# Score products of a differential attention: the low part of q over 64 rows, both softmax halves side by side in two PSUM banks

## The chip, the cores and the metric

The kernel runs on one core of one Trainium2 chip. The metric is the device time of one execution in microseconds (us); lower is better. TensorE (PE, with its weight loader PEld), VectorE (DVE), ScalarE (ACT), GpSimd (POOL) and SyncE (SP, which issues nearly all DMAs) work side by side, each through its own stream of instructions, in the order that was fixed when the kernel was compiled.

## The reference

One layer of a hybrid decoder trunk with 1024 tokens and a width of 1024. A combined input projection gives q, k, v, a convolution branch and gates. The part that matters here is the differential attention, with 8 heads, each with two softmax halves of 64 dimensions, and v of 128:

```python
q = rms_norm(q.reshape(B, S, N_HEADS, 2, HEAD_DIM), q_norm_w[l])
k = rms_norm(k.reshape(B, S, N_HEADS, 2, HEAD_DIM), k_norm_w[l])
...
def probs(qb, kf):
    s = jnp.einsum('bhqd,bhkd->bhqk', qb, kf) * scale + bias
    s = jnp.where(causal, s, -jnp.inf)
    return jax.nn.softmax(s, axis=-1)

p = probs(qb1, k1f) - lamf * probs(qb2, k2f)
return jnp.einsum('bhqk,bhkd->bhqd', p, vf)
```

Behind it come a norm, the convolution branch, the gated merge, an output projection and a SwiGLU feed-forward part, all in float32.

## The kernel before

Every large product is made from rounded operands: a value is split into a high part (what the fast float32 type of TensorE holds) and a low part (the residual), and the product is the sum of high x high, high x low and low x high (`mm3`, L152 to L155, out tiles `pg`, `pW`, `wo`).

The work has stages. Up to about 328 us the first input projections run (V, U, the first Q items). From 328 to about 834 us the attention runs: for each head h and each block i of 128 queries `scores(h, i)` (L865) makes the scores of (i+1) x 128 keys for both halves, `turn` (L903) transposes the probabilities of the step before, `weigh` (L924) multiplies them with v. Between these, `more` issues the remaining projections (Q and G items, tiles `pg`) as filling work, `slot` issues the later parts of earlier steps, and `bg.step` gives VectorE a few taps of the convolution (L542). From 834 us on follow the two branch projections, the output projection and the feed-forward part.

The order of instructions on each engine is set by a planner at compile time: it goes through the program in order of priority, and an instruction whose buffer or operand is not yet there (by the planner's own estimate of times) is passed by later ones that are ready.

Layout of q and k. `q_item` projects one head's q and k, and `turn_qk` (L737) transposes 512 tokens of each, so that the 128 rows of a tile hold the 64 dimensions of the first half and the 64 of the second. L751 writes the high parts into `s1`, L753 the low parts into `lo`. DMAs from SBUF to SBUF (L754, L760, L761, L759 for q; L754, L764, L765 for k) then move rows:

- for k, `s1` becomes [high of half 1; low of half 1] and `s2` [low of half 2; high of half 2], 64 rows each;
- for q, `s1` becomes the high part of half 1 twice, `s2` the high part of half 2 twice, and `lo` and `lo2` the same for the low parts.

So one product over all 128 rows gives (q high) x (k high + k low), and a second one (q low) x (k high + k low). `scores` makes a tile `sc` for each half j and each chunk of at most 512 keys: L883 is the product with q's high part, L884 adds the one with q's low part, and L885 on VectorE adds the bias, writes the sum to `E` and keeps the running minimum. There are three PSUM banks for `sc`. Behind the chunks of one half comes its exponential on ScalarE (L890), and behind both halves VectorE's L896 to L900 combine them. The chunks of the eight blocks are

```python
SPLITS = [[128], [256], [384], [512], [512, 128], [512, 256], [512, 384], [512, 512]]
```

which makes 12 chunks for each head and half, 192 tiles in all.

Other TensorE lines that the prediction names: L693 is a small product over 33 rows (rows of the bias table), L236 eight transposes of 31 rows (the convolution's weights), L673 the projection of v, L744 the transposes of q and k.

Of the kernel before, what the change touches and what calls it, by code (L numbers as in the profile page):

```python
# [10 lines left out]
F32 = mybir.dt.float32  # L11
F32R = mybir.dt.float32r
AF = mybir.ActivationFunctionType
# [3 lines left out]
P = 128  # L17
S = 1024
D = 1024
H = 8  # L20
HD = 64
# [36 lines left out]
def kernel(  # L58
# [28 lines left out]
    dve, act, pool, pe = nc.vector, nc.scalar, nc.gpsimd, nc.tensor  # L87
# [24 lines left out]
    def nm(s):  # L112
        uid[0] += 1
        return f"{s}_{uid[0]}"

    def f32(ap):
        return ap.bitcast(F32)
# [4 lines left out]
    last_lo, last_mm = [None], [None]  # L122
# [16 lines left out]
    def pg():  # L139
        npg[0] += 1  # L140
        p_, tag = pgs[npg[0] % len(pgs)]
        return p_.tile([P, 512], F32, tag=tag, name=nm("pg"))
# [4 lines left out]
    def pm(z="pm"):  # L147
        npm[0] += 1
        p_, tag = pms[npm[0] % len(pms)]
        return p_.tile([P, 512], F32, tag=tag, name=nm(z))  # L150
# [28 lines left out]
    one = ap.tile([1, P], F32, name="one", bufs=1)  # L179
# [14 lines left out]
    def pcol(key, k=0):  # L194
        c = col[key] + k
        return pvec[:, c : c + 1]
# [143 lines left out]
    def gemm_T(w, mhi, mlo, sb, amid=None):  # L340

        o = pg()
        cs = slice(sb * 512, (sb + 1) * 512)
        for k in range(NKT):
            mm3(o[:], w[0][:, k, :], w[1][:, k, :], kt(mhi, k)[:, cs], kt(mlo, k)[:, cs], k == 0, k == NKT - 1)
            if amid is not None and k == NKT // 2 - 1:
                amid()
        return o

    def gemm_N(o, halves, shi, slo, i):  # L350

        ts = slice(i * P, (i + 1) * P)
        for k in range(NKT):
            whi, wlo = halves[k // 4]
            mm3(o, kt(shi, k)[:, ts], kt(slo, k)[:, ts], whi[:, k % 4, :], wlo[:, k % 4, :], k == 0, k == NKT - 1)
# [265 lines left out]
    def rstd_of(ss, n, scale, fast=False):  # L621
        v = sm.tile([P, 16], F32, tag="v", name=nm("v"))[:, :n]
        dve.tensor_scalar(v, ss, scale, EPS, op0=ALU.mult, op1=ALU.add)
        return rsq(v, n, fast)
# [81 lines left out]
    def qk_pool():  # L706

        if not pools:
            vw_ctx.close()
            pools["qk"] = qk_ctx.enter_context(tc.tile_pool(name="qkp", bufs=2, side="right", reuse_waits="tile"))  # L710
        return pools["qk"]

    def q_item(h):
        qkp = qk_pool()
        halves = [ws.next(), ws.next()]
        t = {}
        T[h] = t
        for b in range(2):
            raw = qkp.tile([P, 4, 256], F32, tag="qkraw", name=nm("qkraw"), bufs=2)
            ss = sm.tile([P, 16], F32, tag="ss16", name=nm("ss16"))  # L720
            for i2 in range(2):
                o = pg()
                for e in range(2):
                    gemm_N(o[:, 256 * e : 256 * (e + 1)], halves, hT_hi, hT_lo, 4 * b + 2 * i2 + e)
                act.copy(raw[:, 2 * i2 : 2 * i2 + 2, :], o[:].rearrange("p (e c) -> p e c", c=256))
                jk = sm.tile([P, VD], F32, tag="jk", name=nm("jk"), bufs=1)[:, :HD]
                for g in range(8):
                    act.activation(  # L728
                        jk, o[:, g * HD : (g + 1) * HD], AF.Square, accum_out=ss[:, 8 * i2 + g : 8 * i2 + g + 1]
                    )  # L730
                if i2 == 0:
                    yield
            r = rstd_of(ss[:], 16, 1.0 / HD, fast=h > 0)
            r4 = raw[:].rearrange("p i (g d) -> p (i g) d", d=HD)
            dve.tensor_tensor(r4, r4, r.unsqueeze(2).to_broadcast([P, 16, HD]), op=ALU.mult)

            def turn_qk(b=b, raw=raw):  # L737


                dma = nc.sync.dma_start  # L740
                for z, key in enumerate(("q", "k")):
                    pt = pm("pQ")
                    for i in range(4):
                        pe.transpose(pt[:, i * P : (i + 1) * P], raw[:, i, z * P : (z + 1) * P], ident[:])  # L744
                    w = pcol(key + "n")

                    def part(j):
                        return qkp.tile([P, 512], F32R, tag=f"{key}s{j}", name=f"{key}s{j}_{h}_{b}", bufs=2 if key == "q" else 3)

                    s1, s2 = part(1), part(2)  # L750
                    act.activation(s1[:], pt[:], AF.Identity, scale=w)  # L751
                    lo = part(3) if key == "q" else qkp.tile([P, 512], F32R, tag="klo", name=f"klo_{h}_{b}", bufs=1)
                    dve.scalar_tensor_tensor(lo[:], pt[:], w, f32(s1[:]), op0=ALU.mult, op1=ALU.subtract)  # L753
                    dma(f32(s2[HD:, :]), f32(s1[HD:, :]))  # L754
                    if key == "q":
                        lo2 = part(4)
                        for one, two in ((s1, s2), (lo, lo2)):
                            if one is lo:
                                dma(f32(two[HD:, :]), f32(one[HD:, :]))  # L759
                            dma(f32(two[:HD, :]), f32(one[HD:, :]))  # L760
                            dma(f32(one[HD:, :]), f32(one[:HD, :]))  # L761
                        t["q", b] = (s1, lo), (s2, lo2)
                    else:
                        dma(f32(s2[:HD, :]), f32(lo[HD:, :]))  # L764
                        dma(f32(s1[HD:, :]), f32(lo[:HD, :]))  # L765
                        t["k", b] = s1, s2

            late.append((NT * h if b and h else 0, turn_qk))
            yield

# [71 lines left out]
    aps = at_ctx.enter_context(tc.tile_pool(name="attn", bufs=2, reuse_waits="tile"))  # L842
    psc = at_ctx.enter_context(tc.tile_pool(name="psc", bufs=1, space=PSUM))
    pms.extend([(ps, "pm"), (psc, "pm2")])

    SPLITS = [[128], [256], [384], [512], [512, 128], [512, 256], [512, 384], [512, 512]]
# [18 lines left out]
    def scores(h, i):  # L865

        t, tb = T[h], TB[h]
        nk = (i + 1) * P
        mn = sm.tile([P, 2], F32, tag="mn", name=nm("mn"))
        l = sm.tile([P, 2], F32, tag="l", name=nm("l"))  # L870
        E = []
        qs = slice(i % 4 * P, (i % 4 + 1) * P)
        for j in range(2):
            qh, ql = t["q", i // 4][j]
            e = aps.tile([P, S], F32, tag="E", name=nm("E"), bufs=4)
            E.append(e)
            c0 = 0
            for w in SPLITS[i]:
                ks = slice(c0, c0 + w)
                o = psc.tile([P, 512], F32, tag="sc", name=nm("sc"), bufs=3)  # L880
                kb = c0 // 512
                k = t["k", kb][j][:, :w]
                pe.matmul(o[:, :w], qh[:, qs], k, start=True, stop=False)  # L883
                last_mm[0] = pe.matmul(o[:, :w], ql[:, qs], k, start=False, stop=True).ins  # L884
                dve.tensor_tensor_reduce(  # L885
                    e[:, ks], o[:, :w], tb[:, S - nk + c0 : S - nk + c0 + w], 1.0,
                    mn[:, j : j + 1] if c0 else 3.0e38, ALU.add, ALU.min, accum_out=mn[:, j : j + 1],
                )
                c0 += w
            act.activation(  # L890
                e[:, :nk], e[:, :nk], AF.Exp, bias=mn[:, j : j + 1], scale=-1.0, accum_out=l[:, j : j + 1]
            )
        if h not in RL:
            RL[h] = sm.tile([P, NT], F32, tag="rl1", name=f"rl1_{h}")
        c = sm.tile([P, 1], F32, tag="rl", name=nm("rl"))
        dve.reciprocal(c[:], l[:, 1:2])  # L896
        dve.scalar_tensor_tensor(c[:], c[:], neglam[:], l[:, 0:1], op0=ALU.mult, op1=ALU.mult)
        e1, e2 = E[0][:, :nk], E[1][:, :nk]
        dve.scalar_tensor_tensor(e1, e2, c[:], e1, op0=ALU.mult, op1=ALU.add)
        dve.reciprocal(RL[h][:, i : i + 1], l[:, 0:1])  # L900
        ES[h, i] = E[0]

# [232 lines left out]
    part = bp.tile([P, P], F32, tag="part", name="part", bufs=1)  # L1135
# [50 lines left out]
    for c in range(NE, NKT):  # L1186
        w = ws.next()
# [6 lines left out]
    for cl in ((0, 1, 2), (3, 4), (5, 6), (7,)):  # L1194
        pair = [(c, ws.next()) for c in cl]
        for sb in range(2):
            cs = slice(sb * 512, (sb + 1) * 512)
            for c, w in pair:
# [3 lines left out]
                o = gemm_T(w, cT_hi, cT_lo, sb)  # L1202
# [50 lines left out]
    def wo_bank(t_):  # L1253
        p_, tag = wo_banks[t_]
        return p_.tile([P, 512], F32, tag=tag, name=nm("wo"))
# [8 lines left out]
    for z, (c, ls) in enumerate(WO):  # L1264
        ts_ = [4 * l + i for l in ls for i in range(4)]
        o = {t_: wo_bank(t_) for t_ in ts_}
# [321 lines left out]
```

## Time and profile before

| | |
|---|---|
| Three runs, median (lowest to highest) | 1788.25 us (1786.38 to 1788.89) |
| Profiled execution, span | 1789.3 us, 25085 instructions; no other time of this execution is given |
| TensorE busy in the span | 1753.9 us (98%), 8987 products |
| TensorE weight loads | 1490.4 us (83%) |
| VectorE | 1271.3 us (71%) |
| ScalarE | 804.0 us (45%) |
| Mean granted TensorE clock | 0.991 |
| DMA | 274.77 MB |

A busy time of TensorE counts each product until its modelled end, and successive products overlap; the step from one start to the next tells what a product costs the stream. L12 means line 12 of the kernel. In a row of the time line stand the start, the duration, the engine, the line, the operation, the tiles (out<-in) and the shapes; `64*128` would be a stationary operand of 64 rows and 128 columns. A bracket at the end of a row gives the idle time in front and what ended it; "issue" means that nothing in the profile shows what the engine waited for. In the views of one line or tile stand the number of instructions, durations in ns (lowest/median/highest), and the first and last start.

### The profile page before, as it was taken

The numbers are of one execution on the slowest core, as the hardware profiler recorded it, in microseconds if no ns is written. First come the engines' busy times: TensorE is split into PE (matmuls) and PEld (weight loads), VectorE is DVE, ScalarE is ACT, GpSimd is POOL, SyncE is SP. The second block draws the span as 40 slices with busy tenths as digits, with TensorE's granted clock in tenths as the row PEclk, the third lists the DMA queues.
The fourth block names the chain that finished last, engine by engine and source line by source line (L and its number), as shares of the span: only waits on it lengthen the run. The fifth ranks groups of instructions, "written<-read, shape, count | busy, mean of one in ns | idle before, by whom it ended". The sixth has DMA issues, their size and how long they took to land.

```text
span 1789.3 us, 25085 instructions
## 1 busy us (share of the span) xinstructions
PE 1753.9 (98%) x8987; PEld 1490.4 (83%) x8987; DVE 1271.3 (71%) x2189; ACT 804.0 (45%) x1890; POOL 19.6 (1%) x93
## 2 busy tenths in 40 slices
PE   7899999999999999999999999999999999999999
PEld 5687898988989998987788888878888888888887
DVE  5349888999989898888488533876666766664554
ACT  4221142458767686655447313543333333333333
POOL 0001000000000000000000000000000000000000
PEclk9999999999999999998999999999999999999999
DMA  5337324234343444351793543315454454597663
GB/s 189 97 120 251 118 81 138 73 108 126 109 124 112 131 113 121 98 165 65 258 307 123 165 171 125 117 60 171 143 171 156 154 178 151 184 347 261 219 212 130
DMA packets 249817, 274.77 MB, mean 154 GB/s; under 512 B 16362, under 2 KB 165907, under 8 KB 249692
## 3 DMA queue, kind: packets, MB, share of 16 engines
q1 hardware_dynamic: 248122, 267.47, 46.6%
q0 software_dynamic: 1280, 4.91, 0.9%
q8 instruction: 71, 1.16, 0.3%
q10 hardware_dynamic: 290, 0.79, 0.1%
q14 instruction: 54, 0.44, 0.1%
HBM read 176.07 MB, written 78.68 MB: 142 GB/s over the span
## 4 chain that ended last, share of the span: by engine, by line
PE 90%; DVE 4%; DMA 3%; ACT 2%; issue 1%; SPq 0%; ACTq 0%; DVEq 0%
PE acc L1442 21%; PE pg L153 13%; PE pg L154 13%; PE pg L155 13%; PE acc L468 12%; PE pg L673 5%; PE sc L884 2%; PE wo L155 2%; PE wo L154 2%; PE wo L153 2%; PE sc L883 2%; PE pT L919 1%; PE pW L153 1%; DMA wraw<-in_w_in_dram 1%; PE pW L155 1%
## 5 line engine op out<-in xcount | busy, mean ns | idle before, releaser
L542 DVE SCALAR_TENSOR_TENSOR acc<-u,cw,acc 128x1024 f32<-128x1024 f32 x240 | 306.7, 1278 | 2.5
L153 PE MATMUL pg<-hT_hi,whi 128*128 128x512 f32 x512 | 200.4, 392 | 2.0 <-ACT sgg L580 2.0
L155 PE MATMUL pg<-hT_hi,wlo 128*128 128x512 f32 x512 | 200.9, 393 | 0.0
L154 PE MATMUL pg<-hT_lo,whi 128*128 128x512 f32 x512 | 200.5, 392 | 0.0
L120 ACT CAST whi<-wraw 128x1024 fp32r<-128x1024 f32 x101 | 106.2, 1052 | 188.0 <-PE pg L154 96.5
L125 DVE TENSOR_TENSOR wlo<-wraw,whi 128x1024 fp32r<-128x1024 f32 x101 | 123.1, 1220 | 75.1 <-ACT whi L120 74.8
L125 DVE TENSOR_TENSOR wlo<-draw,whi 128x1024 fp32r<-128x1024 f32 x75 | 91.8, 1224 | 89.0 <-ACT whi L120 83.7
L153 PE MATMUL pg<-whi,hT_hi 128*128 128x256 f32 x512 | 146.3, 286 | 0.0
L154 PE MATMUL pg<-wlo,hT_hi 128*128 128x256 f32 x512 | 145.8, 285 | 0.0
L155 PE MATMUL pg<-whi,hT_lo 128*128 128x256 f32 x512 | 145.7, 285 | 0.0
L120 ACT CAST whi<-draw 128x1024 fp32r<-128x1024 f32 x75 | 79.1, 1055 | 129.5 <-PE acc L468 119.3
L468 PE MATMUL acc<-wlo,whi 128*128 128x512 f32 x308 | 119.8, 389 | 0.0
L468 PE MATMUL acc<-whi,wlo 128*128 128x512 f32 x308 | 119.8, 389 | 0.0
L890 ACT ACTIVATE E<-E,mn 128x256 f32<-128x256 f32 (+7 forms) x128 | 99.5, 779 | 38.8 <-DVE mn L885 37.5
L153 PEld LDWEIGHTS pg<-hT_hi,whi 128*128 128x128 f32 x512 | 96.2, 188 | 21.6 <-ACT sgg L580 2.8
L155 PEld LDWEIGHTS pg<-hT_hi,wlo 128*128 128x128 f32 x512 | 96.2, 188 | 19.9 <-issue 0.6
L154 PEld LDWEIGHTS pg<-hT_lo,whi 128*128 128x128 f32 x512 | 96.2, 188 | 19.4 <-issue 0.6
L153 PEld LDWEIGHTS pg<-whi,hT_hi 128*128 128x128 f32 x512 | 97.6, 191 | 2.1 <-ACT jk L728 0.5
L154 PEld LDWEIGHTS pg<-wlo,hT_hi 128*128 128x128 f32 x512 | 97.6, 191 | 1.4
L155 PEld LDWEIGHTS pg<-whi,hT_lo 128*128 128x128 f32 x512 | 97.6, 191 | 0.9
L1442 PE MATMUL acc<-h_hi,whi 128*128 128x512 f32 x240 | 93.4, 389 | 0.0
L1442 PE MATMUL acc<-h_lo,whi 128*128 128x512 f32 x240 | 93.4, 389 | 0.0
(281 smaller groups left out, 4216.8 us busy)
## 6 DMA issues: line engine op xcount, KB each, us to landing
wraw<-in_w_gate_up_dram SPq DMA_DIRECT2D x44, 512.0 KB, 5.0
wraw<-in_w_in_dram SPq DMA_DIRECT2D x38, 512.0 KB, 3.7
qs<-qs SPq DMA_DIRECT2D x96, 128.0 KB, 2.3
wd<-in_w_down_dram SPq DMA_DIRECT2D x44, 256.0 KB, 3.2
tdT<-wd SPq DMA_DIRECT2D x88, 128.0 KB, 4.4
draw<-sdS SPq DMA_DIRECT2D x44, 256.0 KB, 4.0
draw<-tdT SPq DMA_DIRECT2D x44, 256.0 KB
wraw<-in_w_in_dram SPq DMA_DIRECT2D x32, 256.0 KB, 3.5
```

What stands on the lines that cost most here:

```text
L120: act.copy(dst, src)
L125: last_lo[0] = dve.tensor_tensor(dst, src, f32(hi), op=ALU.subtract).ins
L153: pe.matmul(o, lh, rh, start=start, stop=False)
L154: pe.matmul(o, lh, rl, start=False, stop=False)
L155: last_mm[0] = pe.matmul(o, ll, rh, start=False, stop=stop).ins
L468: m = pe.matmul(o[s_][i][:], l_[:, ts], r_[:, 512:], start=start and j + y_ == 0, stop=j == n - 1 and y_ == 2, skip_group_check=not start,)
L542: dve.scalar_tensor_tensor(acc[0][:], us[c][:, t : t + S], cw[:, c, t : t + 1], acc[0][:], op0=ALU.mult, op1=ALU.add)
L673: last_mm[0] = pe.matmul(o[:], l_, r_, start=n_ == 0, stop=n_ == len(terms) - 1).ins
L883: pe.matmul(o[:, :w], qh[:, qs], k, start=True, stop=False)
L884: last_mm[0] = pe.matmul(o[:, :w], ql[:, qs], k, start=False, stop=True).ins
L890: act.activation(e[:, :nk], e[:, :nk], AF.Exp, bias=mn[:, j : j + 1], scale=-1.0, accum_out=l[:, j : j + 1])
L1442: pe.matmul(o[:], a_[x_][:, k, :], b_[y_][:, k, :], start=start and k + x_ + y_ == 0, stop=k == 3 and x_ == 1, skip_group_check=not start,)
```

## The change

The product with q's low part now runs over 64 rows: `lo` keeps the low part of half 1 in rows 0 to 63 and that of half 2 in rows 64 to 127, as L753 writes it, and it is multiplied with the 64 rows of the k tile that hold k's high part (rows 0 to 63 of `s1`, rows 64 to 127 of `s2`). The product low x low is no longer formed. The tile `lo2` and three DMAs for each q tile go. In `scores` the loops are exchanged: for each chunk both halves' tiles are taken, first the two products with the high part, then the two with the low part, then VectorE's two L885; the two exponentials come behind all chunks.

```diff
                     dve.scalar_tensor_tensor(lo[:], pt[:], w, f32(s1[:]), op0=ALU.mult, op1=ALU.subtract)
                     dma(f32(s2[HD:, :]), f32(s1[HD:, :]))
                     if key == "q":
-                        lo2 = part(4)
-                        for one, two in ((s1, s2), (lo, lo2)):
-                            if one is lo:
-                                dma(f32(two[HD:, :]), f32(one[HD:, :]))
-                            dma(f32(two[:HD, :]), f32(one[HD:, :]))
-                            dma(f32(one[HD:, :]), f32(one[:HD, :]))
-                        t["q", b] = (s1, lo), (s2, lo2)
+                        dma(f32(s2[:HD, :]), f32(s1[HD:, :]))
+                        dma(f32(s1[HD:, :]), f32(s1[:HD, :]))
+                        t["q", b] = (s1, s2), lo
...
-        E = []
+        E = [aps.tile([P, S], F32, tag="E", name=nm("E"), bufs=4) for j in range(2)]
         qs = slice(i % 4 * P, (i % 4 + 1) * P)
-        for j in range(2):
-            qh, ql = t["q", i // 4][j]
-            e = aps.tile([P, S], F32, tag="E", name=nm("E"), bufs=4)
-            E.append(e)
-            c0 = 0
-            for w in SPLITS[i]:
-                ks = slice(c0, c0 + w)
-                o = psc.tile([P, 512], F32, tag="sc", name=nm("sc"), bufs=3)
-                kb = c0 // 512
-                k = t["k", kb][j][:, :w]
-                pe.matmul(o[:, :w], qh[:, qs], k, start=True, stop=False)
-                last_mm[0] = pe.matmul(o[:, :w], ql[:, qs], k, start=False, stop=True).ins
+        qh, ql = t["q", i // 4]
+        rows = slice(0, HD), slice(HD, P)
+        c0 = 0
+        for w in SPLITS[i]:
+            o = [psc.tile([P, 512], F32, tag="sc", name=nm("sc"), bufs=3) for j in range(2)]
+            k = t["k", c0 // 512]
+            for j in range(2):
+                pe.matmul(o[j][:, :w], qh[j][:, qs], k[j][:, :w], start=True, stop=False)
+            for j in range(2):
+                last_mm[0] = pe.matmul(
+                    o[j][:, :w], ql[rows[j], qs], k[j][rows[j], :w], start=False, stop=True
+                ).ins
+            for j in range(2):
                 dve.tensor_tensor_reduce(
-                    e[:, ks], o[:, :w], tb[:, S - nk + c0 : S - nk + c0 + w], 1.0,
+                    E[j][:, c0 : c0 + w], o[j][:, :w], tb[:, S - nk + c0 : S - nk + c0 + w], 1.0,
                     mn[:, j : j + 1] if c0 else 3.0e38, ALU.add, ALU.min, accum_out=mn[:, j : j + 1],
                 )
-                c0 += w
-            act.activation(
-                e[:, :nk], e[:, :nk], AF.Exp, bias=mn[:, j : j + 1], scale=-1.0, accum_out=l[:, j : j + 1]
-            )
+            c0 += w
+        for j in range(2):
+            e = E[j][:, :nk]
+            act.activation(e, e, AF.Exp, bias=mn[:, j : j + 1], scale=-1.0, accum_out=l[:, j : j + 1])
```

## The prediction

> **What bounds the kernel now.** I read the page first, then the table by stages, the score tile's own view, the time line of TensorE around single score products, and last the few places where TensorE already runs a product over fewer than 128 rows.
>
> ```profile
> span 1789.3 us, 25085 instructions
> ...
> PE 90%; DVE 4%; DMA 3%; ACT 2%; issue 1%; SPq 0%; ACTq 0%; DVEq 0%
> ```
>
> ```profile
> 64.90:66.00 1.10, 1.07 (x9) 1.01 (x9) 0.65 (x2) 0.00 (x0) 0.00 (x0) 0.50 0.06 24
> ...
> 328.00:834.00 506.00, 499.04 (x3344) 454.86 (x3344) 452.77 (x1039) 339.94 (x1171) 11.28 (x63) 1.00 0.40 116
> ```
>
> The second table gives, for each stage, its length, the busy time of PE, PEld, DVE, ACT and POOL, the granted clock, and DMA. Nine tenths of the chain that ended last is TensorE. The scores lie in the attention stage, 328 to 834 us, where TensorE is busy for 499.0 of 506.0 us at the full clock and VectorE for 452.8. So TensorE has some 7 us of visible idle time there, VectorE 53 us: what the change adds to or takes from TensorE's stream goes to the end nearly one for one, and what it adds to VectorE or ScalarE has room.
>
> ```profile
> L883 PE MATMUL sc<-ks,qs x192: 220/389/792, 329.4 to 833.5; 128*128 128x512 f32 x96, 128*128 128x128 f32 x32, 128*128 128x256 f32 x32, 128*128 128x384 f32 x32
> ...
> L884 PE MATMUL sc<-ks,qs x192: 222/388/628, 329.5 to 834.1; 128*128 128x512 f32 x96, 128*128 128x128 f32 x32, 128*128 128x256 f32 x32, 128*128 128x384 f32 x32
> L885 DVE CUSTOM_DVE_ANT_0 E<-sc,tb x128: 279/680/693, 331.6 to 833.4; 128x512 f32<-128x512 f32 x80, 128x128 f32<-128x128 f32 x16, 128x256 f32<-128x256 f32 x16, 128x384 f32<-128x384 f32 x16
> ...
>   DMA qs<-qs: 0.7, 2
> ```
>
> There are 192 score tiles, so 96 pairs (first and second softmax half of one chunk of keys), half of them 512 keys wide. The durations in these rows (0.39 us) overlap one another; what a product costs the stream is the step from its start to the next start:
>
> ```profile
> 329.42 0.22 PE L883 MATMUL sc<-ks,qs 128*128 128x128 f32 x1
> 329.48 0.28 PE L884 MATMUL sc<-ks,qs 128*128 128x128 f32 x1
> 329.60 0.27 PE L883 MATMUL sc<-ks,qs 128*128 128x128 f32 x1
> 329.71 0.27 PE L884 MATMUL sc<-ks,qs 128*128 128x128 f32 x1
> ```
>
> ```profile
> 512.40 0.39 PE L883 MATMUL sc<-ks,qs 128*128 128x512 f32 x1
> 512.62 0.39 PE L884 MATMUL sc<-ks,qs 128*128 128x512 f32 x1
> 512.86 0.40 PE L153 MATMUL pg<-hT_hi,whi 128*128 128x512 f32 x1
> ...
> 514.46 0.39 PE L883 MATMUL sc<-ks,qs 128*128 128x512 f32 x1
> 514.69 0.39 PE L884 MATMUL sc<-ks,qs 128*128 128x512 f32 x1
> 514.92 0.39 PE L154 MATMUL pg<-hT_lo,whi 128*128 128x512 f32 x1
> ```
>
> The step is 0.23 us for 512 keys and 0.11 us for 128; between them I estimate 0.17 for 384 and 0.12 for 256. Over 96 pairs (48 of 512, 16 of each other width) the mean is (48 x 0.23 + 16 x 0.40) / 96 = 0.18 us.
>
> The two extracts also show the order of the stream. In the first, two tiles follow each other, hi, lo, hi, lo. In the second, two tiles lie 2 us apart and TensorE works on the projection (pg) between them. There are three banks for score tiles, VectorE empties them when its queue gets there, and the compiled order puts a tile's first product where a bank comes free and its second right behind. I counted all 384 score products in the trace: hi and lo of one tile are neighbours in 184 of 192, but of 96 pairs of successive tiles within a step only 28 follow each other with nothing between, the first at 329.42 and the last at
>
> ```profile
> 826.41 0.48 PE L883 MATMUL sc<-ks,qs 128*128 128x512 f32 x1
> ```
>
> **The change, part by part.** Gained on paper: the low-part products read 64 rows each, the first half rows 0 to 63, the second rows 64 to 127. If two such products run side by side, a pair costs one step for its low parts in place of two; if they run one behind the other, it costs the same as now. The number of products and of weight loads stays at 384. So the gain lies between 0 and 0.18 us a pair, 17.3 us for 96 pairs, and only pairs that stay neighbours can have it.
>
> What is paid for it is the switch between a product over all rows and one over some. The trace has such places:
>
> ```profile
> 140.41 0.39 PE L154 MATMUL pg<-hT_lo,whi 128*128 128x512 f32 x1
> 140.73 0.81 PE L693 MATMUL pm<-oh,rb 33*8 33x384 f32 x2
> 141.47 0.50 PE L155 MATMUL pg<-hT_hi,wlo 128*128 128x512 f32 x1
> 141.80 0.39 PE L153 MATMUL pg<-hT_hi,whi 128*128 128x512 f32 x1
> ```
>
> ```profile
> L693 PE MATMUL pm<-oh,rb x6: 482/483/487, 134.8 to 141.1; 33*8 33x384 f32 x6
> ```
>
> ```profile
> 140.73 0.10 PEld L693 LDWEIGHTS pm<-oh,rb 33*8 33x8 f32 x2 [0.35 <-issue]
> 141.47 0.19 PEld L155 LDWEIGHTS pg<-hT_hi,wlo 128*128 128x128 f32 x1 [0.64 <-issue]
> ```
>
> Into the 33-row product the step is 140.73 - 140.41 = 0.32 instead of 0.23: 0.09 us lost. The second of the two L693 starts at 140.73 + 0.81 - 0.48 = 141.06, a step of 0.33; the step out of it is 141.47 - 141.06 = 0.41, 0.08 lost; and the first full product takes 0.33 instead of 0.23, 0.10 more, since its weights were not loaded ahead: the weight loader stands idle for 0.64 us, and load and product start together. In sum 141.80 - 140.41 = 1.39 us against 0.23 + 0.33 + 0.33 + 0.23 = 1.12: 0.27 us for one visit, with weights of only 8 columns. Our low parts have 128 columns, so their load, which may not start before the array is empty either, costs about what the full one did, 0.11 us (the step of the 128-wide products, which is all load). One visit: 0.27 + 0.11 = 0.38 us. Bounds: 0.27 if that load is hidden, 0.49 if it costs twice that.
>
> It is not the plain fp32 type of these helper products that costs this. The full-array fp32 transposes show nothing of it:
>
> ```profile
> 772.82 1.03 PE L744 MATMUL pQ<-ident,qkraw 128*128 128x128 f32 x8
> 773.61 0.47 PE L154 MATMUL pg<-hT_lo,whi 128*128 128x512 f32 x1
> 773.92 0.40 PE L155 MATMUL pg<-hT_hi,wlo 128*128 128x512 f32 x1
> ```
>
> From 772.82 to 773.92 are 1.10 us, just eight steps of 0.11 and one of 0.23. And products with few rows but all 128 columns pay it too:
>
> ```profile
> L236 PEld LDWEIGHTS pm<-ident,cwrow x8: 177/219/219, 64.9 to 65.6; 31*128 31x128 f32 x8
> ```
>
> ```profile
> 65.91 0.29 PEld L673 LDWEIGHTS pg<-vwh,hT_hi 128*128 128x128 f32 x1
> ```
>
> Eight 31-row loads start between 64.9 and 65.6, 0.1 us apart; the first full load behind them starts only at 65.91, 0.3 us after the eighth. These 0.2 us lost are at the half clock (0.50 in the table above), so some 0.1 at the full one. Few rows alone suffice.
>
> The Trainium skill speaks against the change here: "TensorEngine Tiling (Array Packing)", section Tiling Modes, Key Properties, says that a change of tiling mode, not of the tile within a mode, drains TensorE. It gives no figure; the rows above agree that something is emptied (0.09 in, 0.08 out), and by this rule alone, without the loads, the sum below would be 164 x 0.17 = 28 us. On the gain, the same skill's "TensorE: Matmul & The Clock Gate", Part 3, says that products in different row groups start about 4 ns apart, which by its figure would make a pair kept together gain its full step; no row here shows two such products side by side.
>
> How many visits? In the new order hi and hi come first, then lo and lo. But the second hi needs a second bank. Where that bank is not free yet, the first lo, which is ready, goes first, then projection products, then the second hi and lo: the pair makes two visits, and nothing runs side by side. I take the present counts, as the banks (three) and what empties them (L885, 0.68 us each, behind VectorE's other work) stay: 28 pairs with one visit, 68 with two, 28 + 136 = 164 visits.
>
> - Visits: 164 x 0.38 = 62.3 us more on TensorE.
> - Side by side in 28 pairs: between 0 and 28 x 0.18 = 5.0 us less. The nearest row is the load step: if the second load comes 0.11 us behind the first, a pair gains 0.18 - 0.11 = 0.07: 2.0 us less.
> - TensorE's waits in the stage, 506.0 - 499.0 = 7 us: what it now waits for will be ready when it comes later. Between 0 and 7; I take 4 us less.
> - DMAs: of six moves for each q tile three go (the residual's three, 48 in all), each 0.5 to 0.6 us on SP's queue, ahead of the k moves, the value loads and the weight loads that SP issues behind them.
>
> ```profile
> L760 SPq DMA_DIRECT2D qs<-qs x32: 467/592/1670, 263.7 to 785.1; - x32
> L761 SPq DMA_DIRECT2D qs<-qs x32: 461/462/536, 266.1 to 790.5; - x32
> ```
>
>   TensorE's own wait for them is 0.7 us (the row of the score tile's view); what queues behind them is worth between 0 and 5 us; I take 1 us less, the nearest being that row.
> - The exponentials of both halves now come behind both halves' minima, so VectorE's reciprocal waits longer for the second one.
>
> ```profile
> DVE rl L896 <- ACT E L890: 15.9, 15, 2.7
> ```
>
>   That wait is 15.9 us now. One exponential more in front of each of 64 reciprocals, at most 2.7 us (the longest such wait), mostly filled by other work, stays in VectorE's 53 us of room and the time that TensorE adds; I take 0, up to 10 us if the cover is gone. The freed residual tile gives room that nothing uses: 0.
>
> Sum: 62.3 - 2.0 - 4 - 1 = +55.3 us. Against the profiled execution's own 1789.3 us that is 1844.6; the runs' median, 1788.25, lies 1.05 us lower (the three runs lie from 1786.38 to 1788.89, so the span leaves no room for anything around it), which makes 1843.5 us. The forecast's own range: with 0.27 a visit 164 x 0.27 = 44.3, less 5 for side by side and 5 for waits and DMAs, +34 (1822); with no pair kept together and 0.41 a visit 192 x 0.41 = +78 (1866).
>
> **Rivals.** *Pairs stay together.* If the planner places both banks' products at once, there are 96 visits: 96 x 0.38 = 36.5, less 96 x 0.07 = 6.7, less 5: +25, 1813 us; with the full side-by-side gain of 17.3 it is 1803. For it speaks that 184 of 192 hi-lo neighbours stayed together; against it that only 28 of 96 tile neighbours did.
>
> *TensorE blocks on the second bank.* Pairs kept together, but at the price of a wait for one L885, 0.68 us, in the 68 pairs that lack a bank: 25 + 46 = +71, 1859 us. Queued behind the waiting product would be all projection work. Against it: the compiled order fills such places now, and TensorE's waits total 7 us.
>
> *Faster: no switch cost.* If fp32r products over 64 rows need neither an emptied array nor late loads (all rows quoted for the switch are plain fp32), a visit costs 0 and the neighbours run side by side: 5.0 in 28 pairs plus 1 for DMAs, 1782 us; with all 96 kept together 17.3 + 5, 1766. The point from which it decides: 5.0 + 1 over 164 visits, a visit under 0.04 us. Against it: 0.27 measured at L693, and L236.
>
> *Nothing to be seen.* A visit near 0.04 us, 1788.
>
> **How the numbers follow.** Forecast 0.62, pairs together 0.17, blocking 0.09, faster 0.09, nothing 0.03. A measurement of this kernel tells about 0.2% (3.6 us) from no change. Slower by more: 0.62 + 0.17 + 0.09 = 0.88; same 0.03; faster 0.09. The range reaches from the second case's lower end, 1803, to the forecast's upper end, 1866; it leaves out the faster case and some tails, about 0.2.
>
> **What the profile after would show.** L884's successor's steps: rows with 64*128 in place of 128*128, a load that starts with its product instead of ahead of it, 0.3 us before the first 64-row product where 0.23 stood, and 0.3 us for the full product behind it. Low parts of a pair apart, with pg between them, in about two thirds of the pairs. The attention stage near 560 us in place of 506, the other stages unchanged, VectorE's busy time the same. 48 fewer moves of qs. Wrong would be: a 64-row product with its load ahead and no longer step around it (the faster case), or nearly all low parts back to back (pairs together).

## The result and the profile after

The changed kernel takes 1837.41 us (median of 4 runs, 1834.43 to 1837.78) against 1788.57 us before (4 runs, 1786.38 to 1789.05): ratio 1.0271, 95% interval 1.0256 to 1.0285. It is 48.8 us slower; forecast were 55.3. The profiled spans differ by 1835.5 - 1789.3 = 46.2 us, and the following accounts are made against that. The other 2.6 us lie in the profiled execution of the kernel before, which was a slower one: its mean granted clock is 0.991, where that of this kernel's runs beside the experiments is 0.992 to 0.996. In those runs the time is about 1.8 us longer than the span, so this execution took some 1791 us.

The page after, its span and its chain, and the attention stage, which now runs from 328 to 884 us (columns of the stage table as in the prediction):

```profile
span 1835.5 us, 25001 instructions
...
PE 93%; DVE 2%; ACT 2%; DMA 2%; issue 1%; SPq 0%; ACTq 0%
```

```profile
328.00:884.00 556.00, 551.60 (x3344) 453.66 (x3342) 459.39 (x1042) 340.63 (x1171) 11.23 (x63) 1.00 0.32 95
```

TensorE's share of the chain went from 90 to 93%. The stage runs the same number of products (3344) in 556 us instead of 506; VectorE and ScalarE work about as long as before (452.8 and 339.9 us). Mark by mark, the changed kernel is 0.3 us ahead when the first score product starts and 46.1 us behind once the attention is over, and stays at 46.1 to the end. All of the loss is in this stage.

The score tile's view after: L876 is the high part, L878 the low part, now 64*128.

```profile
L876 PE MATMUL sc<-ks,qs x192: 220/392/505, 329.2 to 881.4; 128*128 128x512 f32 x96, 128*128 128x128 f32 x32, 128*128 128x256 f32 x32, 128*128 128x384 f32 x32
L878 PEld LDWEIGHTS sc<-ks,qs x192: 182/183/183, 329.4 to 881.9; 64*128 64x128 f32 x192
L878 PE MATMUL sc<-ks,qs x192: 322/466/502, 329.4 to 881.9; 64*128 64x512 f32 x96, 64*128 64x128 f32 x32, 64*128 64x256 f32 x32, 64*128 64x384 f32 x32
...
  issue: 33.9, 128
```

The low part got longer, not shorter: 466 ns in the middle against 388 before. And in front of these products engines stood idle 128 times with nothing in the profile that they waited for ("issue"). The time line of TensorE and of its weight loader around one pair shows what that is:

```profile
513.25 0.40 PE L876 MATMUL sc<-ks,qs 128*128 128x512 f32 x1
513.58 0.49 PE L878 MATMUL sc<-ks,qs 64*128 64x512 f32 x1
514.00 0.50 PE L155 MATMUL pg<-hT_hi,wlo 128*128 128x512 f32 x1
514.34 0.39 PE L153 MATMUL pg<-hT_hi,whi 128*128 128x512 f32 x1
```

```profile
513.02 0.19 PEld L876 LDWEIGHTS sc<-ks,qs 128*128 128x128 f32 x1
513.58 0.18 PEld L878 LDWEIGHTS sc<-ks,qs 64*128 64x128 f32 x1 [0.37 <-issue]
514.00 0.19 PEld L155 LDWEIGHTS pg<-hT_hi,wlo 128*128 128x128 f32 x1 [0.24 <-issue]
514.11 0.19 PEld L153 LDWEIGHTS pg<-hT_hi,whi 128*128 128x128 f32 x1
```

Three products of 512 columns take 514.34 - 513.25 = 1.09 us, where three steps of 0.23 are 0.69: 0.40 us for one visit to the 64-row shape. It falls into 0.10 before it, 0.19 within and 0.11 behind. The loads at 513.58 and 514.00 start together with their products, those at 513.02 and 514.11 ahead of them. Over all 140 visits of a single product the mean is 0.404 us (the mean step within, and the medians 0.097 in front and 0.105 behind). Around a product of 128 columns it is less, about 0.29.

A pair whose low parts stayed neighbours:

```profile
348.73 0.72 PE L876 MATMUL sc<-ks,qs 128*128 128x512 f32 x2
349.38 0.51 PE L878 MATMUL sc<-ks,qs 64*128 64x512 f32 x2
349.81 0.38 PE L153 MATMUL pg<-whi,hT_hi 128*128 128x256 f32 x1
```

Two 64-row products span 0.51 us, one alone 0.49 to 0.50: they run side by side. In the trace the second starts 3 ns behind the first, and the step out is the same 0.43. So the gain that the change was to bring exists, in 26 of the 96 pairs.

### The profile page after: what moved, and what is told of

It reads as the page before. It is cut to its first block, busy times and chain, and to the rows that moved or that the text cites. A ratio compares the mean times of both kernels' runs of the same rounds, so it can differ in the third digit from the quotient of the medians.

```text
span 1835.5 us, 25001 instructions
## 1 busy us (share of the span) xinstructions
PE 1803.3 (98%) x8987; PEld 1486.8 (81%) x8987; DVE 1276.2 (70%) x2189; ACT 804.8 (44%) x1890; POOL 19.5 (1%) x93
## 4 chain that ended last, share of the span: by engine, by line
PE 93%; DVE 2%; ACT 2%; DMA 2%; issue 1%; SPq 0%; ACTq 0%
PE acc L1439 21%; PE pg L155 13%; PE pg L153 13%; PE pg L154 13%; PE acc L468 11%; PE pg L673 4%; PE sc L878 3%; PE sc L876 2%; PE pT L916 2%; PE wo L155 2%; PE wo L153 2%; PE wo L154 2%; PE pW L153 1%; PE pW L154 1%; PE pW L155 1%; DMA wraw<-in_w_in_dram 1%
## 5 line engine op out<-in xcount | busy, mean ns | idle before, releaser
L153 PE MATMUL pg<-hT_hi,whi 128*128 128x512 f32 x512 | 202.4, 396 | 0.0
L153 PE MATMUL pg<-whi,hT_hi 128*128 128x256 f32 x512 | 148.1, 289 | 0.0
L153 PEld LDWEIGHTS pg<-hT_hi,whi 128*128 128x128 f32 x512 | 96.2, 188 | 21.7 <-issue 2.7
L154 PEld LDWEIGHTS pg<-hT_lo,whi 128*128 128x128 f32 x512 | 96.2, 188 | 21.1 <-issue 2.6
L153 PEld LDWEIGHTS pg<-whi,hT_hi 128*128 128x128 f32 x512 | 97.6, 191 | 4.7 <-issue 3.0
L882 DVE CUSTOM_DVE_ANT_0 E<-sc,tb 128x512 f32<-128x512 f32 (+3 forms) x128 | 73.9, 586 | 32.4 <-PE pT L916 14.5
```

The lines of the kernel that those rows point to most:

```text
L153: pe.matmul(o, lh, rh, start=start, stop=False)
L154: pe.matmul(o, lh, rl, start=False, stop=False)
L882: dve.tensor_tensor_reduce(E[j][:, c0 : c0 + w], o[j][:, :w], tb[:, S - nk + c0 : S - nk + c0 + w], 1.0, mn[:, j : j + 1] if c0 else 3.0e3 ...
```

## The experiments

I call a run of 64-row products with nothing between them a visit. To compare the kernels I took the same stretch of work in each trace (from the 270th to the 1260th start at L153, which takes in the attention) and split its length: the plain sum of the steps of all full-row products (0.227 us for 512 columns, 0.171, 0.120, 0.110 for 384, 256, 128 and for transposes), the visits (from the first 64-row product's start to the next full one's, plus 0.097 in front and 0.105 behind, the medians), and the rest, which I call waiting. (Taken over the attention stage alone, the waiting before is 13.8 us, the figure in the expectations.) The last column tells for how much of the stretch TensorE was granted the half clock.

| kernel | stretch, us | full-row steps | visits | waiting | at half clock, us |
|---|---|---|---|---|---|
| before | 633.0 | 608.6 | 0 | 24.4 | 13.7 |
| after | 679.3 | 574.0 | 96.4 (166) | 8.9 | 3.4 |
| order only | 625.7 | 608.6 | 0 | 17.1 | 3.4 |
| rows only | 697.0 | 574.0 | 110.1 (192) | 12.9 | 6.8 |
| pairs together | 653.6 | 574.0 | 58.5 (100) | 21.1 | 13.7 |
| low part twice | 653.2 | 643.2 | 0 | 10.0 | 3.4 |
| first half's rows | 660.5 | 591.3 | 54.7 (96) | 14.5 | 6.8 |
| four banks | 672.5 | 608.6 | 0 | 63.9 | 27.3 |
| four banks, one visit a step | 694.1 | 574.0 | 50.5 (70) | 69.6 | 47.8 |

The waiting is a remainder, and not all of it is TensorE waiting for others. One of the pieces at half clock, in the kernel before (columns of the stage table as in the prediction):

```profile
841.70:848.30 6.60, 6.34 (x28) 5.97 (x29) 2.44 (x4) 2.51 (x9) 0.00 (x0) 0.50 0.00 0
```

Products of 256 columns start 0.21 us apart there (844.91 and 845.13) and 0.12 us apart behind it (848.84 and 848.96); in most such pieces the median step is 1.77 or 1.78 times the plain one. So about 0.44 us of waiting stand in the table for each us at half clock: some 6 of the 24.4 us before, 1.5 of the 8.9 after. What lowers the clock no run here varies; its mean differs between runs of one kernel too (0.992 to 0.996 before), and the table has one execution of each.

Theory: each visit costs TensorE 0.40 us. Rival: the new order does it (banks taken in pairs, late exponentials).

**Order only** (label e1_order_only): the new loops, the low part over all rows.

```diff
...
-                    o[j][:, :w], ql[rows[j], qs], k[j][rows[j], :w], start=False, stop=True
+                    o[j][:, :w], ql[j][:, qs], k[j][:, :w], start=False, stop=True
```

> The changed kernel's loops and order (high, high, low, low; minima and exponentials of both halves behind), but the low-part products go over all 128 rows, with the low parts of q doubled by moves as in the kernel before. No product over 64 rows, so no visit. Theory (each visit to the 64-row shape costs TensorE 0.40 us, the order costs nothing): 1784 to 1793 us, as before. Rival (the order, the banks taken in pairs and the late exponentials make the loss): at least half of it stays, 1812 us or more.

Measured: 1783.35 us (11 runs), ratio 0.9975, interval 0.9966 to 0.9983. The whole loss is gone, and the kernel is 0.25% faster than before, a little more than the theory's lower end allowed; the rival falls.

**Rows only** (e2_rows_only): the loops of before, the low part over 64 rows.

```diff
...
-                last_mm[0] = pe.matmul(o[:, :w], ql[:, qs], k, start=False, stop=True).ins
+                last_mm[0] = pe.matmul(o[:, :w], ql[rows, qs], k[rows], start=False, stop=True).ins
```

> The kernel before with its own loops and order (high, low of one half, its exponential, then the other half), but the low-part products go over 64 rows and the three moves of the low part are left out. Compiled order: 192 visits, none of two products. Theory: 192 x 0.40 = 77 us more on TensorE, less some 13 us of waits that it covers: 1845 to 1860 us, slower than the changed kernel. Rival (the order is to blame): under 1805 us.

Measured: 1857.41 us, ratio 1.0389 (1.0371 to 1.0407). The 64 rows alone, in the old order, cost 69 us, more than the change as a whole. (The execution in the table is the quickest of the four, 1852.38 us.)

**Pairs together** (e3_pairs_together):

```diff
-                pe.matmul(o[j][:, :w], qh[j][:, qs], k[j][:, :w], start=True, stop=False)
-            for j in range(2):
+                high = pe.matmul(o[j][:, :w], qh[j][:, qs], k[j][:, :w], start=True, stop=False).ins
+            with tc.issue_after(high):
+                for j in range(2):
...
```

> The changed kernel, with both low parts of a pair queued behind the second high part, so that a pair stays together: 100 visits in the compiled order, 92 of them with two products. Theory: 100 x 0.40 = 40 us, less 92 x 0.18 = 17 us for products that run side by side, less about 10 us of covered waits: 1795 to 1812 us, still slower than before. Rival (TensorE blocks on the second bank): 1840 us or more. Rival (low parts run one behind the other): 1812 to 1822 us.

Measured: 1809.14 us, ratio 1.0118 (1.0103 to 1.0134): 28 us less than the changed kernel (in the table 38 us less in visits, 12 given back as waiting, of which some 4.5 are half clock), and still slower than before. TensorE does not block on the second bank. Its pairs run as the one above at 348.73 us does (for 512 columns the median steps are 3 ns and 0.43 us). Even with the pair kept together the visit loses: a pair saves one step, at most 0.23 us, and pays 0.40. What I expected wrongly was 10 us of covered waits; the table has 24.4 - 21.1 = 3.3.

**First half's rows** (e5_first_half_rows): about as many visits, but each with one product.

```diff
...
                 pe.matmul(o[j][:, :w], qh[j][:, qs], k[j][:, :w], start=True, stop=False)
-            for j in range(2):
-                last_mm[0] = pe.matmul(
-                    o[j][:, :w], ql[rows[j], qs], k[j][rows[j], :w], start=False, stop=True
-                ).ins
+                r = rows[0] if j == 0 else slice(0, P)
+                last_mm[0] = pe.matmul(o[j][:, :w], ql[j][r, qs], k[j][r, :w], start=False, stop=True).ins
```

> The first half's low part goes over 64 rows, the second half's over all 128 (its low part doubled by two moves); each low part directly behind its own high part. Compiled order: 96 visits of one product, nothing side by side. Theory: 96 x 0.40 = 38 us, less 10 to 13 us of covered waits: 1810 to 1818 us, so 10 to 17 us above the kernel with pairs kept together, which makes about as many visits: that is what side by side earns. Rival (64-row products of different halves run one behind the other): no more than 4 us above it.

Measured: 1815.54 us, ratio 1.0151 (1.0136 to 1.0166), 6.4 us above the pairs kept together, between theory and rival. The table explains it: side by side saves 591.3 + 54.7 - 574.0 - 58.5 = 13.5 us of TensorE's time. But the kernel with pairs kept together has 21.1 - 14.5 = 6.6 us more of waiting, and that takes half of the saving back; some 3 of the 6.6 are half clock (13.7 us of it against 6.8).

**Low part twice** (e4_low_twice): an addition of known size, without visits.

```diff
+                pe.matmul(o[:, :w], ql[:, qs], k, start=False, stop=False)
                 last_mm[0] = pe.matmul(o[:, :w], ql[:, qs], k, start=False, stop=True).ins
```

> The kernel before with each low-part product issued twice (the low part counts double, so the scores are not the reference's). It adds 192 full-row products, 34.6 us of steps, and no visit. It measures how much of an addition to TensorE in the attention stage reaches the end. If the stage's waits (13.8 us above the plain sum of steps) are covered by it: 1806 to 1814 us. If nothing is covered: 1819 to 1824 us.

Measured: 1811.99 us, ratio 1.0137 (1.0123 to 1.0151). Of 34.6 us added, some 24 reach the end. The waiting falls by 14.4, from 24.4 to 10.0; some 4.5 of that is less half clock, so about 10 us of waits are covered. This is the cover that my sum had too small.

**Moves back** (e6_moves_back): three moves for each q tile, into a tile that nothing reads.

```diff
+                        lo2 = part(4)
+                        dma(f32(lo2[HD:, :]), f32(lo[HD:, :]))
+                        dma(f32(lo2[:HD, :]), f32(lo[HD:, :]))
+                        dma(f32(lo2[HD:, :]), f32(lo[:HD, :]))
```

> The changed kernel with three moves for each q tile put back, into a tile that nothing reads. It measures what the 48 moves are worth. Theory: 0 to 2 us above the changed kernel, 1836 to 1840 us. Rival (they delay what queues behind them on SP's queue): 3 to 6 us above it.

Measured: 1837.93 us (1837.59 to 1842.45), ratio 1.0282 (1.0267 to 1.0298) beside 1.0271 for the changed kernel. The intervals overlap, and the compiled order has 168 visits in place of 166: a worth of the 48 moves cannot be told from zero here, and 3 us or more are not seen in the medians (49.4 us above the kernel before, against 48.8).

**Four banks** (e7_four_banks) and **one visit a step** (e8_one_visit): can more products in a visit pay for it? That takes a fourth bank. It is taken from the three that the transposes share with the product with v (`pW`).

```diff
-    pms.extend([(ps, "pm"), (psc, "pm2")])
...
-                o = psc.tile([P, 512], F32, tag="sc", name=nm("sc"), bufs=3)
+                o = psc.tile([P, 512], F32, tag="sc", name=nm("sc"), bufs=4)
```

> The kernel before with four PSUM banks for the score tiles; the fourth is taken from the transposes. It is the base for the next kernel. Theory: 1784 to 1796 us, as TensorE hardly waits for banks. Rival (the bank taken from the transposes is missed): over 1796 us.

Measured: 1828.82 us, ratio 1.0231 (1.0214 to 1.0248): the theory's figure falls, the bank is missed (waiting 63.9 us, some 12 of it half clock; the mean granted clock of the four runs is 0.988, against 0.993 before). On this base, all high parts of a step before all its low parts (shown against the changed kernel):

```diff
...
-                last_mm[0] = pe.matmul(
-                    o[j][:, :w], ql[rows[j], qs], k[j][rows[j], :w], start=False, stop=True
-                ).ins
...
+        with tc.issue_after(high):
+            for j, c0, w, o, k in chunks:
+                last_mm[0] = pe.matmul(o[:, :w], ql[rows[j], qs], k[rows[j]], start=False, stop=True).ins
...
```

> Four banks as in the kernel before it, and all high parts of a step (both halves, both chunks) before all its low parts over 64 rows: 70 visits in the compiled order, 27 of them with four products and 35 with two. Theory: 70 x 0.40 = 28 us less about 16 us for side by side, less some 8 us of covered waits: 0 to 10 us above the base with four banks. If a visit's cost grows with its products (loads one behind the other): 10 to 25 us above the base.

Measured: 1850.12 us, ratio 1.0341 (1.0323 to 1.0358), 21.3 above its base. That is inside the second figure, but not for its reason. One visit of four, on TensorE and its loader:

```profile
657.63 0.40 PE L877 MATMUL sc<-ks,qs 128*128 128x512 f32 x1
657.96 0.73 PE L882 MATMUL sc<-ks,qs 64*128 64x512 f32 x4
658.62 0.39 PE L153 MATMUL pg<-whi,hT_hi 128*128 128x256 f32 x1
658.85 0.28 PE L154 MATMUL pg<-wlo,hT_hi 128*128 128x256 f32 x1
```

```profile
657.96 0.30 PEld L882 LDWEIGHTS sc<-ks,qs 64*128 64x128 f32 x4 [0.25 <-issue]
```

From 657.63 to 658.85 are 1.22 us, where six plain products (five of 512 columns, one of 256) take 1.25: this visit of two pairs pays for itself, just. In the 27 visits of four the second and the fourth product start 3 to 4 ns behind their partners (medians), and the third 0.333 us behind the second, not 0.227. But the four loads start at -2, 2, 107 and 110 ns from the first product, so the third load runs while the first product is still under way, 0.23 us ahead of its own product, and the step out of the visit is then short: 0.32 us for 512 columns, where a visit of one or two products has 0.43. The 0.11 for a load that starts together with its product is paid once in a visit, here inside it, there at its end. The visit does not grow with its rounds. It costs the same 0.40 and saves two steps: 0.86 against 0.91 us of plain products where both chunks have 512 columns, 0.81 against 0.80 with 384 in the second one, 0.75 against 0.69 with 256 (medians, with the 0.20 around the visit).

So the sum of the theory holds for the visits: 70 x 0.40 = 28 us, less 17 for the steps saved, is 11; the table has 574.0 + 50.5 - 608.6 = 15.9, of which some 4 are waits inside four of the visits. The rest of the 21.3 us is waiting: the theory took off 8 us for covered waits, the table has 5.7 us more than the base, with TensorE at half clock for 47.8 us against 27.3, which is some 9 us. The runs agree: their mean granted clock is 0.982 against 0.988, at most 10 us of the span.

**Late exponentials** (e9_late_exp) and **order of chunks** (e10_chunk_order) ask what made the order-only kernel faster. The first moves only L890 of the kernel before behind both halves; the second is the order-only kernel with each low part directly behind its high part.

```diff
-            act.activation(
-                e[:, :nk], e[:, :nk], AF.Exp, bias=mn[:, j : j + 1], scale=-1.0, accum_out=l[:, j : j + 1]
-            )
+        for j in range(2):
+            e = E[j][:, :nk]
+            act.activation(e, e, AF.Exp, bias=mn[:, j : j + 1], scale=-1.0, accum_out=l[:, j : j + 1])
```

> The kernel before with one edit: the two exponentials of a step come behind both halves' minima, as in the changed kernel; all products over 128 rows. It asks which part of the new order made the order-only kernel 0.25% faster. If the late exponentials do it: 1782 to 1785 us. If the order of the chunks does it: 1787 to 1791 us.

```diff
                 pe.matmul(o[j][:, :w], qh[j][:, qs], k[j][:, :w], start=True, stop=False)
-            for j in range(2):
                 last_mm[0] = pe.matmul(
```

> The order-only kernel, but each tile's low part directly behind its high part again; both halves of a chunk before the next chunk, exponentials behind, all products over 128 rows. If the order of chunks and exponentials makes the gain: 1782 to 1785 us, as the order-only kernel. If taking high, high, low, low makes it: 1787 to 1791 us.

Measured: 1788.19 us, ratio 0.9997 (0.9988 to 1.0006), and 1785.82 us, ratio 0.9983 (0.9974 to 0.9992). Late exponentials make no difference that can be told from zero. The second kernel lies between its two expected figures: the order of the chunks gives some of the gain and high, high, low, low perhaps the rest; the intervals of this kernel and of the order-only one overlap (0.9974 to 0.9983). A part of the gain is the clock. In the same stretch TensorE is at half clock for 13.7 us before and with late exponentials, 10.2 with the order of chunks, 3.4 in the order-only kernel. Over the runs of the two kernels the mean granted clock is 0.9939 before and 0.9950 in the order-only kernel, about 2 of its 4.8 us. Why its clock is higher, and which waits go, was not settled.

## Why the prediction was right, step by step

- **The switch is what counts: shown.** Without the 64 rows there is no loss (order only), with them alone there is more of it (rows only). A visit costs 0.404 us against 0.38 forecast; the term taken from the 33-row products (0.09 in, 0.08 and 0.10 out) and the 0.11 for the load both held. The Trainium skill's rule that a change of tiling mode drains TensorE ("TensorEngine Tiling (Array Packing)", Key Properties) agrees, but the drain is half of the price at most: by my split 0.21 to 0.22 us are the two loads that are not made ahead. The visits of four bear the split out: their step out has 0.10 us less than that of a single product, and the 0.11 for the first load stands in the middle of the visit.
- **The number of visits: held.** Forecast 28 pairs together and 136 single visits, 164 in all; the trace has 26 and 140, 166. Bank by bank, the order of before was a good guide. 166 x 0.404 = 67.1 us, forecast 62.3.
- **Side by side: mis-sized.** I took 0.07 us a pair from the load step (2.0 us); it is the full step, 3 ns between starts, 26 x 0.20 = 5.2 us, the upper bound. The Trainium skill's "TensorE: Matmul & The Clock Gate", Part 3, gives about 4 ns between such starts, and the 3 ns here agree.
- **Covered waits: mis-sized, and outside its bounds.** I capped them at the 7 us of visible idle time and took 4. The table has 24.4 - 8.9 = 15.5 us, of which some 4.5 are clock (13.7 us at half clock before, 3.4 after) and some 11 waits. Busy times of TensorE overlap by 0.17 us a product, so short waits do not show as idle time: in the same stretch TensorE's idle time is 10.3 us before and 7.5 after. Only the sum of steps shows them. The low part issued twice shows that an addition alone, in the old order, covers about 10; how much of the changed kernel's 11 comes with its order instead was not told apart (the order-only kernel's waiting is 7.3 us lower, some 4.5 of it clock).
- **Moves and exponentials: not contradicted.** 1 us and 0 forecast; the moves put back and the late exponentials moved alone give nothing that can be told from zero. VectorE's wait for the exponentials is where it was:

```profile
DVE rl L893 <- ACT E L889: 16.4, 19, 3.2
```

The sum with the measured terms: 67.1 - 5.2 - 15.5 = 46.4 us, the spans' difference 46.2. As the waiting is the remainder of the stretch, this only shows that nothing lies outside it. That the forecast came within 9 us of it is in part luck: the visits came out 4.8 us dearer, which hid a part of what side by side (3.2 us) and waiting (11.5 us) took off beyond their terms. One reading was wrong without harm: the profiled span of 1789.3 us was no measure of the time before, as the slower execution it belongs to shows; the forecast time was made from the median.

Of the rivals, "pairs stay together" is what the planner doesn't do by itself; forced, it took 1809 us, against 1813 with my terms. Blocking on the second bank did not come. "No switch cost" is refuted by the first two experiments.

## What to carry to other kernels

In these runs a product over 64 rows is no shorter by itself; it pays only side by side with another one, and each change between full rows and fewer costs a nearly fixed time (here 0.40 us there and back), so it has to be shared. One pair in a visit does not pay for it, two pairs of 512 columns just do, and the bank that this took cost far more. Count visits in the order of instructions, not in the source: here, with three banks, the planner took 70 of 96 pairs apart. And measure the slack of a busy TensorE by the sum of start-to-start steps, with the granted clock beside it: a stage that looked 98.6% busy, with 7 us idle, had 13.8 us above its plain steps.

The fastest version measured is the order-only one, 1783.35 us, a quarter of a per cent below the kernel before.

## What the runs showed of the hardware that I had not expected

- Two 64-row products on different rows start 3 ns apart and take the time of one, for widths from 128 to 512; a 64-row load takes 183 ns, a full one 189.
- Behind each change of shape the first load starts together with its product, the next one 0.11 us later, and the second step is late by as much: 0.333 us in place of 0.227 within the 64-row shape, 0.105 us more among full rows. After that loads are ahead again, within the 64-row shape too: in the visits of four the load for rows in use starts 0.23 us ahead of its product.
- TensorE is granted half the clock for pieces of 3.4 to 10.2 us in the compared stretches (before: 831.3 to 838.1 and 841.6 to 848.4 us), and its busy time hardly shows it (6.34 of 6.60 us in the row above).
- Taking one PSUM bank from the transposes and `pW` cost 40 us, at most 10 of them by the granted clock (0.988 in place of 0.993). In the waits of that kernel's attention stage, ScalarE's wait for transposes (who waited, for what, us in total, times, longest) stands at 46.0 us, where the same view of the kernel before has 24.9:

```profile
ACT ph L120 <- PE pT L919: 46.0, 37, 3.3
```
